# A row-maximum kernel whose ten long loads are each split into two transfers on two DMA queues

## The chip, the cores and the metric

The kernel runs on one core of a Trainium2 chip. The metric is the device time of one execution in microseconds (us); the median of three runs counts.

A core has a matrix engine (TensorE, PE in the profile), a vector engine (VectorE, DVE), an activation engine (ScalarE, ACT), a general engine (GpSimd, POOL) and an engine for synchronization (SyncE, SP). They run side by side and wait for each other by semaphores. Data comes from the main memory (HBM) into the on-chip memory (SBUF, 128 partitions) by 16 DMA engines. A transfer is handed to them by an instruction of some engine; the transfers of SP stand in one queue, those of ScalarE in another.

## What is computed

The maximum of each of 32 x 512 rows of 1024 floats:

```python
def setup_inputs():
    batch, seq, dim = 32, 512, 1024
    return {"x": np.random.randn(batch, seq, dim).astype(np.float32)}

def reference(x):
    return np.max(x, axis=-1).astype(np.float32)
```

The input has 67.1 MB and is read once. The output has 64 KB.

## The kernel before

**Tiling.** The 16384 rows are laid over 128 partitions, so each partition has 128 rows. In what follows "a row" is one row on each of the 128 partitions: 128 x 1024 floats, 512 KB. The rows come in loads of `n` rows each (`BLOCKS`, line 13): loads 0 to 10 have 2, 15, 16, 14, 11, 11, 10, 10, 8, 8 and 7 rows, loads 11 to 17 have 3, 3, 3, 2, 1, 1 and 1. The last two rows come in two pieces of columns each (`PIECES`, line 26), four transfers. Within a load each partition reads one contiguous run of `n` x 4 KB.

**The ring.** Loads go into a ring of 47 rows (`RING`, line 17) in SBUF, one after another. A load that does not fit before the end begins at the ring's start (line 112). So load 4 takes the place of loads 0 and 1, loads 5 and 6 the rest of load 1 and part of load 2, load 7 that of loads 2 and 3, load 8 that of load 4, load 9 that of loads 4 and 5, load 10 that of loads 5 and 6.

**The order.** `PLAN` (line 31) writes out the steps by hand. `dN` reduces load N on VectorE (`direct`, line 184, through `maximum`, line 77, one instruction at line 78); `pN` reduces a part of the columns of some rows (`partial`); `tN` and `bN` send the other columns another way: PE transposes them into PSUM (line 160), ScalarE copies them out (line 166), GpSimd reduces over the partitions (line 168), PE transposes the result back (line 178); `mN` merges the two; `fN` reduces a piece. Only some rows of loads 10, 13, 14 and 17 go that way (`SHARED`, line 20), so PE, ScalarE and GpSimd have work only near the end.

Before each step `issue()` (line 231) hands over all loads whose place in the ring has no reader left in the plan; `readers` (line 222) counts the steps that still read each load. The waits themselves are put in by the framework: a transfer waits until the reduce that read its place has finished. It also waits for an earlier transfer with the same completion semaphore; transfers take eight such semaphores in turn. When all loads are handed over, the four pieces follow (line 243).

All loads and pieces are issued from SP, in this order. On ScalarE there are a table load, the six copies of line 166 and at the end two transfers that store the result (lines 265 and 267).

Of the kernel before, what the change touches and what calls it, by code (L numbers as in the profile page):

```python
# [40 lines left out]
def kernel(  # L41
# [5 lines left out]
    nc = tc.nc  # L47
# [29 lines left out]
    def maximum(out, in_):  # L77
# [8 lines left out]
        out=colno, data0=ident, data1=ident, initial=-1.0, op0=ALU.add, op1=ALU.mult))  # L86
    in_turn("DVE", nc.vector.transpose(out=rowno, in_=colno[:, :32]))  # L87
    for q in range(1, P // 32):
        part = rowno[q * 32:(q + 1) * 32, 0:1]
        in_turn("DVE", nc.vector.tensor_scalar(  # L90
            out=part, in0=part, scalar1=float(q * 32), scalar2=None, op0=ALU.add))
    identity = in_turn("DVE", nc.vector.tensor_scalar(  # L92
        out=ident, in0=colno, scalar1=rowno[:, 0:1], scalar2=None, op0=ALU.is_equal))
# [41 lines left out]
    def rows(j):  # L135
        start, n, _, _ = loads[j]
        return ring[:, I + start * D:I + (start + n) * D].rearrange("p (i d) -> p i d", d=D)
# [90 lines left out]
    issued = 0  # L228
    behind = None

    def issue():
        nonlocal issued
        while issued < len(loads):
            start, n, src, _ = loads[issued]
            if any(readers[j] and s < start + n and start < s + k
                   for j, (s, k, _, _) in enumerate(loads[:issued])):
                return
            load = nc.sync.dma_start(out=rows(issued), in_=src)  # L238
            issued += 1
        if any(readers[j] and s < at + last + 1 and at < s + k for j, (s, k, _, _) in enumerate(loads)):  # L240
            return
        while pieces:
            nc.sync.dma_start(out=pieces[0][0], in_=pieces[0][1])
            pieces.pop(0)

    for step in PLAN:
        issue()
        kind, k = step[0], int(step[1:])
        if kind in "dp":
            (direct if kind == "d" else partial)(k)  # L250
            readers[k] -= 1
        elif kind == "t":
            turn(k)
            readers[chunks[k][0]] -= 1
        elif kind == "b":
            back(k)
        elif kind == "m":
            merge(k)
        else:
            inst = maximum(*tail[k])  # L260
            if behind is None:
                behind = inst
# [34 lines left out]
```

## Time and profile before

| | |
|---|---|
| median of 3 runs | 163.71 us (163.69 to 163.97) |
| span of the profiled execution, first to last instruction | 162.1 us |
| VectorE busy | 135.3 us |
| VectorE waiting for loads | 23.5 us in 4 waits |
| PE, ScalarE, GpSimd busy | 13.6, 6.3, 15.9 us |
| DMA, mean rate over the span | 414 GB/s |

The page gives no other time for the profiled execution than its span; some 1.6 us lie outside it in the runs. Each engine's groups of instructions are told by the line of the kernel that made them, with the operation and the tiles (`ring<-in_x_dram` is a load). SPq is SP's sequencer issuing transfers. The profile's times count from the first instruction of the span.

```profile
ring<-in_x_dram SPq DMA_DIRECT2D x1, 7680.0 KB, 22.6
ring<-in_x_dram SPq DMA_DIRECT2D x1, 7168.0 KB, 58.0
```

These two lines list transfers: load 1 (7680 KB) landed 22.6 us after its issue, load 3 (7168 KB), which stands two places behind it in the same queue, 58.0 us after.

### The profile page before, as it was taken

To read this page: it belongs to the slowest core of one execution; us is meant where nothing else is said; L and a number is where in the kernel's file an instruction comes from. 1 tells how busy PE (TensorE), PEld (TensorE's weight loads), DVE (VectorE), ACT (ScalarE), POOL (GpSimd) and SP (SyncE) were. 2 spreads that over 40 slices of the span, in tenths; PEclk is the share of its full clock that TensorE was granted. 3 is DMA by queue.
4 is the path that set the end of the run, shared out by engine and by line. 5 is a ranking of instruction groups with operands and counts; after the bars stand their busy time and mean duration, and the time that the engine had idled before them with its cause. 6 is when DMAs were issued, how large, how long until landed. Compare 5 with 4: busy or idle time off the path is not lost.

```text
span 162.1 us, 295 instructions
## 1 busy us (share of the span) xinstructions
PE 13.6 (8%) x76; PEld 11.7 (7%) x76; DVE 135.3 (83%) x33; ACT 6.3 (4%) x7; POOL 15.9 (10%) x10
## 2 busy tenths in 40 slices
PE   0000000000000000000000000000000000772942
PEld 0000000000000000000000000000000000762731
DVE  3500019998399999999999999996999999999994
ACT  3000000000000000000000000000000000241120
POOL 0000000000000000000000000000000000099791
PEclk9999999999999999999999999999999999996555
DMA  5995999599879999898999799799999989999991
GB/s 178 566 485 258 470 501 517 259 517 517 354 340 439 453 404 534 356 523 367 478 411 475 334 485 475 334 485 388 477 429 388 466 382 446 415 421 416 411 388 34
DMA packets 3456, 67.18 MB, mean 414 GB/s; under 512 B 640, under 2 KB 896, under 8 KB 1536
## 3 DMA queue, kind: packets, MB, share of 16 engines
q1 hardware_dynamic: 3168, 67.11, 96.8%
q10 hardware_dynamic: 288, 0.07, 0.2%
HBM read 67.11 MB, written 0.07 MB: 414 GB/s over the span
## 4 chain that ended last, share of the span: by engine, by line
DMA 50%; DVE 47%; SPq 1%; issue 0%; DVEq 0%
DMA ring<-in_x_dram 50%; DVE ring L78 45%; DVE joint L78 2%; SPq L238 1%; DVEq L292 0%
## 5 line engine op out<-in xcount | busy, mean ns | idle before, releaser
L78 DVE TENSOR_REDUCE ring<-ring 128x1 f32<-128x1024 f32 (+13 forms) x20 | 129.9, 6547 | 23.5 <-DMA ring<-in_x_dram 23.5
L168 POOL PARTITION_ALL_REDUCE top<-sb x6 | 15.7, 2658 | 142.6 <-ACT sb L166 142.5
L160 PE MATMUL ps<-ident,ring 128*128 128x128 f32 x38 | 9.0, 423 | 140.0 <-DMA ring<-in_x_dram 140.0
L160 PEld LDWEIGHTS ps<-ident,ring 128*128 128x128 f32 x38 | 7.6, 225 | 140.1 <-issue 140.1
L166 ACT COPY sb<-ps 128x1024 f32<-128x1024 f32 (+2 forms) x6 | 5.0, 834 | 150.5 <-PE ps L160 143.5
L78 DVE TENSOR_REDUCE joint<-ring 128x2 f32<-128x1280 f32 (+1 forms) x3 | 3.9, 1314 | 0.0
L178 PE MATMUL got<-ident,top 1*128 1x1 f32 x24 | 2.7, 228 | 3.8 <-POOL top L168 3.6
L178 PEld LDWEIGHTS got<-ident,top 1*128 1x128 f32 x24 | 2.4, 188 | 4.6 <-POOL top L168 4.6
L178 PE MATMUL joint<-ident,top 1*128 1x1 f32 x14 | 2.0, 244 | 1.9 <-POOL top L168 1.9
L178 PEld LDWEIGHTS joint<-ident,top 1*128 1x128 f32 x14 | 1.7, 210 | 2.7 <-POOL top L168 2.7
L166 ACT ACT_TABLE_LOAD x1 | 1.3, 1283 | 0.7 <-PEq L281 0.7
L83 DVE MEMSET ident<- 128x128 f32 x1 | 0.2, 165 | 0.8 <-PEq L281 0.8
L90 DVE TENSOR_SCALAR rowno<-rowno 32x1 f32<-32x1 f32 x3 | 0.4, 146 | 0.1
L85 DVE TENSOR_TENSOR_SCAN colno<-ident 128x128 f32<-128x128 f32 x1 | 0.4, 425 | 0.0
L92 DVE TENSOR_SCALAR ident<-colno,rowno 128x128 f32<-128x128 f32 x1 | 0.3, 288 | 0.0
L87 DVE STREAM_TRANSPOSE rowno<-colno 128x32 f32<-128x32 f32 x1 | 0.2, 211 | 0.0
L78 DVE TENSOR_REDUCE ring<-got 128x3 f32<-128x24 f32 x1 | 0.2, 172 | 0.0
L78 DVE TENSOR_REDUCE ring<-joint 128x5 f32<-128x20 f32 x1 | 0.2, 170 | 0.0
L281 POOL MEMSET const-float32-0.0<- 128x1 f32 x1 | 0.1, 98 | 0.2 <-issue 0.2
L281 POOL MEMSET const-bfloat16-1.0<- 128x1 bf16 x1 | 0.1, 102 | 0.0
L281 POOL MEMSET const-uint8-127<- 128x1 uint8 x1 | 0.1, 101 | 0.0
L281 POOL MEMSET const-float32-1.0<- 128x1 f32 x1 | 0.1, 98 | 0.0
(1 smaller groups left out, 0.1 us busy)
## 6 DMA issues: line engine op xcount, KB each, us to landing
ring<-in_x_dram SPq DMA_DIRECT2D x2, 5632.0 KB, 29.9
ring<-in_x_dram SPq DMA_DIRECT2D x2, 5120.0 KB, 36.8
ring<-in_x_dram SPq DMA_DIRECT2D x2, 4096.0 KB, 32.5
ring<-in_x_dram SPq DMA_DIRECT2D x1, 7680.0 KB, 22.6
ring<-in_x_dram SPq DMA_DIRECT2D x1, 7168.0 KB, 58.0
ring<-in_x_dram SPq DMA_DIRECT2D x3, 1536.0 KB, 35.7
ring<-in_x_dram SPq DMA_DIRECT2D x1, 3584.0 KB, 29.2
ring<-in_x_dram SPq DMA_DIRECT2D x2, 1024.0 KB, 17.8
```

The costliest lines, as they stand in the source:

```text
L78: return in_turn("DVE", nc.vector.reduce_max(out=out, in_=in_, axis=X))
L83: in_turn("DVE", nc.vector.memset(ident, 1.0))
L85: in_turn("DVE", nc.vector.tensor_tensor_scan(out=colno, data0=ident, data1=ident, initial=-1.0, op0=ALU.add, op1=ALU.mult))
L87: in_turn("DVE", nc.vector.transpose(out=rowno, in_=colno[:, :32]))
L90: in_turn("DVE", nc.vector.tensor_scalar(out=part, in0=part, scalar1=float(q * 32), scalar2=None, op0=ALU.add))
L92: identity = in_turn("DVE", nc.vector.tensor_scalar(out=ident, in0=colno, scalar1=rowno[:, 0:1], scalar2=None, op0=ALU.is_equal))
L160: in_turn("PE", nc.tensor.transpose(out=ps[:, w:w + P], in_=rows(j)[:, lead[j] + r + i, c * P:(c + 1) * P], identity=ident,))
L166: in_turn("ACT", nc.scalar.copy(out=sb[:, :W], in_=ps[:, :W]))
L168: in_turn("POOL", nc.gpsimd.partition_all_reduce(top[:, :W], sb[:, :W], P, bass_isa.ReduceOp.max))
L178: in_turn("PE", nc.tensor.transpose(out=share(j)[:, r + i, c:c + 1], in_=tops[k][0:1, w:w + P], identity=ident[0:1, 0:1],))
L238: load = nc.sync.dma_start(out=rows(issued), in_=src)
L281: nc = _bacc.Bacc("TRN2", target_bir_lowering=False, num_devices=1)
```

## The change

A load of more than six rows is issued as two transfers. SP issues the upper rows, `half` to `n`, and ScalarE's queue the lower `half` = `n // 2` rows. Both stand at the same place in `issue()`; the ring, the plan, the reduces and all other transfers stay. Loads 1 to 10 are concerned: SP takes 8, 8, 7, 6, 6, 5, 5, 4, 4 and 4 rows of them, ScalarE's queue 7, 8, 7, 5, 5, 5, 5, 4, 4 and 3. Loads 0 and 11 to 17 and the pieces stay whole on SP.

```diff
-            load = nc.sync.dma_start(out=rows(issued), in_=src)
+            half = n // 2 if n > 6 else 0
+            nc.sync.dma_start(out=rows(issued)[:, half:, :], in_=src[:, half:, :])
+            if half:
+                nc.scalar.dma_start(out=rows(issued)[:, :half, :], in_=src[:, :half, :])
             issued += 1
```

In the built program ScalarE's ten transfers come first in its stream, ahead of the table load and the copies.

## The prediction

> **What bounds the kernel now.** A "row" below is one row of x for each of the 128 partitions: 128 x 1024 floats, 512 KB. The kernel loads 128 of them. I read the busy line of each engine first, then the DMA queues, then the chain of waits, then VectorE's timeline.
>
> ```profile
> PE 13.6 (8%) x76; PEld 11.7 (7%) x76; DVE 135.3 (83%) x33; ACT 6.3 (4%) x7; POOL 15.9 (10%) x10
> q1 hardware_dynamic: 3168, 67.11, 96.8%
> DMA 50%; DVE 47%; SPq 1%; issue 0%; DVEq 0%
> ```
>
> Two things are nearly full: the 16 DMA engines (96.8% of the span by the packets of the one load queue) and VectorE (83%). The chain that ended last is half the one and half the other. The packet count tells how a load is cut: 22 loads make 3168 packets, 144 each, that is 128 of data (one for each partition, so 8 on each of the 16 engines, whatever the length) and 16 small ones that signal the end.
>
> ```profile
> 5.65 2.29 DVE L78 TENSOR_REDUCE ring<-ring 128x2 f32<-128x2048 f32 x1 [3.14 <-DMA ring<-in_x_dram]
> 23.78 16.15 DVE L78 TENSOR_REDUCE ring<-ring 128x15 f32<-128x15360 f32 x1 [15.85 <-DMA ring<-in_x_dram]
> 43.13 66.53 DVE L78 TENSOR_REDUCE ring<-ring 128x16 f32<-128x16384 f32 x5 [3.20 <-DMA ring<-in_x_dram]
> 110.97 40.23 DVE L78 TENSOR_REDUCE ring<-ring 128x10 f32<-128x10240 f32 x7 [1.30 <-DMA ring<-in_x_dram]
> ```
>
> This is the timeline of VectorE (start, length, what; in brackets the idle time before it). VectorE waits for load 0 (2 rows), for load 1 (15 rows), for load 2 (16 rows), then runs five reduces without a gap, waits 1.30 us for load 7, and from 110.97 works nearly without a gap to the end. Between the landings of loads 1 and 2 lie 16 rows and 43.13 - 23.78 = 19.35 us: 1.209 us a row for all engines together, 434 GB/s. All later landings follow from it, since the queue never runs dry.
>
> ```profile
> 43.13 66.55 DVE ring L78 x5
> 111.01 38.94 DMA ring<-in_x_dram
> 149.97 1.22 DVE ring L78
> 158.52 0.05 issue
> 158.57 0.49 DVE ring L78
> 159.05 0.09 issue
> 159.14 0.59 DVE ring L78
> ```
>
> These are pieces of the chain of waits. The last two pieces of data land just as VectorE is ready for them (0.05 and 0.09 us of waiting). So the end is set by both: data landing later ends later, and VectorE running late from load 2 on ends later too, less the 1.30 us before load 7 and these 0.14 us, which are all the slack it has.
>
> **The change part by part.** Loads 1 to 10 (15, 16, 14, 11, 11, 10, 10, 8, 8, 7 rows) become an upper part on SP (8, 8, 7, 6, 6, 5, 5, 4, 4, 4 rows) and a lower one on the Activation queue (7, 8, 7, 5, 5, 5, 5, 4, 4, 3 rows). Bytes, destinations and reduces are the same. In the built program's order the ten Activation transfers stand ahead of everything else on ScalarE.
>
> *Issuing.* SP issues the same 22 transfers; ScalarE issues ten more, at 0.33 to 0.61 us by the rows of L238, some 4 us in all. Queued behind them on ScalarE are the table load (1.28 us, at 0.72 until now) and the six copies of L166, and for these POOL and PE wait. The last Activation transfer (load 10) waits for the reduce of load 6, which ends at 109.67 now and near 118 by the forecast below; the first copy starts at 140.95. So 20 us cover it: cost 0. Without that cover it would be the 1.28 us.
>
> *Waits for semaphores.* Transfers share eight completion semaphores in turn, and each waits for the one eight places before it. With 32 in place of 22, loads 11 to 13 newly wait for load 7's two parts and load 8's upper part; the latest of them, 8's upper part, lands near 125 by the count below, when half of load 9 and loads 10 to 12 (4+7+3+3 = 17 rows, some 20 us) are still queued, so no engine runs dry. The four last pieces wait, as now, for loads 10 to 13. Each reduce waits for two semaphores: an added semaphore instruction is 0.017 us in the rows of L238. Together 0 to 0.1 us; I take 0.
>
> *DMA time.* The records of the packets in the trace give 2267 ns for 61,440 bytes, 1213 for 32,768, 1062 for 28,672 and 160 for 4,096: 27.1, 27.0, 27.0 and 25.6 bytes a ns, back to back. The halves are 12 to 32 KB long, a length that costs nothing. Ten more transfers at 8 packets and some 5 ns are 0.4 us at most, and only if the DMA still sets the end; I take 0. A gain in rate: an engine gives the same 27 whether its packet is 28 or 64 KB, so I see no gap that a second queue fills. Only the start has one. Load 2 ends 33 rows: 43.13 - 33 x 1.209 = 3.23, while the first packet starts at 1.73. At most those 1.5 us of warming up and signalling could be won.
>
> Here the Trainium skill speaks against a gain, and leaves the loss open. DMA: Bandwidth & Descriptors, section "Issuing engines are not separate DMA queues", says that issuing from several engines saves only issue time; on its own it would make this change cost nothing, 163.7. The section "Queues, rings and completion order" adds that an engine takes turns between queues a packet at a time, and that a packet is some 9 to 17 descriptors: with one packet to a descriptor that is the first way below, with a transfer's whole share as one packet it is the third. No run here shows which.
>
> *Order of landing.* This is the term that matters. A load is ready when both parts are; the Activation queue has no part of load 0, so it begins load 1 while SP is at load 0, and is ahead from then on. What it moves ahead is taken from the load that VectorE waits for. One queue only is busy in this trace, so how an engine shares is not shown, and the cost is bounded by the ways it could:
>
> 1. A packet from each queue in turn. Each transfer has 8 packets on an engine, so transfers pair up: load 0 (2 rows) with 1's lower part (7), 1's upper (8) with 2's lower (8), 2's upper (8) with 3's lower (7). Load 1 is complete after 2+7+8+8 = 25 rows instead of 17 and load 2 after 40 instead of 33. Load 1: 23.78 + 8 x 1.209 = 33.45, its reduce ends at 49.60. Load 2: 43.13 + 7 x 1.209 = 51.59, later than that, so it decides. If SP's packet goes first in each turn, the last packet of load 3's lower part (8.46/8 = 1.06 us) falls behind it; I take half of that, 0.53: 51.06. The five reduces take 66.53: 117.6, against 110.97 now, so +6.6; less the 0.14 at the end, **+6.5**.
> 2. Byte by byte. SP has 10 rows to the end of load 1 and 18 to the end of load 2, the other queue moves as many: 20 and 36 rows, each 3 late. +3.63 - 1.30 - 0.14 = +2.2.
> 3. A whole transfer in turn, SP first: 0, 1 lower, 1 upper, 2 lower, 2 upper: 17 and 33 rows, +0.
> 4. All of the Activation queue's first three transfers (22 rows) first: load 1 after 32 rows, 41.9, reduced by 58.07, when load 2 (40 rows) is there: 58.07 - 43.13 - 1.30 - 0.14 = +13.5.
>
> The nearest row is that of the packets themselves, which are recorded one after another at a length of one partition, so I take the first.
>
> *What is late next.* Nothing starves by it: load 4 is issued after load 1's reduce, 49.6, while the 47 rows before it last until 3.2 + 47 x 1.209 = 60; loads 5 and 6 after load 2's, 117.6 - 66.53 + 17.22 = 68.3, while load 4 lasts to 73; load 8 after load 4's, near 95, while load 7 lasts to 111. Later loads are shifted too (load 7 by load 8's lower 4 rows, 4.8 us, to 115.8), but VectorE comes for it at 117.6 only. From there the data is always earlier than VectorE, which sets the end alone.
>
> The sum: 162.1 + 6.5 = 168.6 of span. The runs before have a median of 163.71, 1.6 above the span: **170.2 us**.
>
> **The rivals.** *Byte by byte* (2): 163.71 + 2.2 = 165.9. For it: nothing says that an engine finishes one packet before it begins another queue's. Against: in its one queue no packet overlaps the next. *A whole transfer in turn* (3), the case on the other side: the place is each engine's choice between the two rings, the price 0, 163.7, and it decides if load 0 goes ahead of the other queue's first transfer on all 16 engines; if the other goes first, it becomes case 1. For it: both engines start at 0.72, and load 0 has short packets. Against: it needs all 16 engines alike. *A smaller lead*: if the Activation queue's first packet comes some microseconds after SP's, part of load 0 is done; with 2 of its 8 packets gone the lead is 6 of 8, 5.25 rows: 6.35 - 0.53 - 1.44 = +4.4, 168.1; with 4 gone 3.5 rows, +2.3. *A start-up gain*: up to 1.5 us off loads 1, 2 and 7 alike, with landings otherwise in order, 162.2. *The other queue first* (4): 177.2.
>
> **How the numbers follow.** A measurement of this kernel can tell 0.2% (0.33 us) from no change. Packet by packet with up to two packets of delay (168.1 to 170.9): 0.52, and its own range is that. A smaller lead (166.5 to 168.1): 0.09. Byte by byte (165.3 to 166.5): 0.19. Whole transfers, same time: 0.10. Start-up gain: 0.05. Other queue first: 0.05. The range takes the first three, 0.80: 165.2 to 171.2. Faster 0.05, same 0.10, slower 0.85.
>
> **What would show it.** VectorE's wait before load 1 grows from 15.85 to some 20 (load 0 itself is late, near 12) and load 1 starts near 33; load 2 starts near 51; the wait before load 7 is gone; from load 2 on VectorE has no gap; the load queues together still move 67.11 MB by 159. Starts near 27 and 47 would say byte by byte; 23.8 and 43.1 that nothing moved. The prediction is wrong if load 2 lands by 44.4 (the 1.30 us of slack then swallow it), if VectorE waits for a later load as well, or if the last data lands well ahead of 158.

## The result, and the profile after

The change makes the kernel slower: 171.03 us (median of 4 runs, 170.94 to 171.11) against 163.84 us for the kernel before beside it (163.69 to 163.97). The ratio is 1.0444, with a 95% interval of 1.0431 to 1.0456. The span of the profiled execution went from 162.1 to 169.2 us.

From the page of the kernel after: busy time by engine, the two DMA queues (q1 is SP's, q10 ScalarE's) and the chain that ended last.

```profile
PE 12.6 (7%) x76; PEld 11.0 (6%) x76; DVE 135.0 (80%) x33; ACT 6.3 (4%) x7; POOL 15.9 (9%) x10
q1 hardware_dynamic: 3168, 39.32, 55.1%
q10 hardware_dynamic: 1728, 27.85, 38.6%
DVE 47%; DMA 43%; issue 8%; DVEq 0%; SPq 0%
```

No engine does more work than before. The bytes are the same; q10 carries the ten lower parts and the stores. So the lost time is waiting: 30.8 us of VectorE's waiting for loads, against 23.5 before. (The 8% of "issue" in the chain are not idle time of VectorE, which the profile shows busy without a break from 85 to 150 us.) VectorE's timeline of the kernel after (start, length, what; idle time before it in brackets):

```profile
14.04 2.29 DVE L78 TENSOR_REDUCE ring<-ring 128x2 f32<-128x2048 f32 x1 [11.53 <-DMA ring<-in_x_dram]
33.55 16.15 DVE L78 TENSOR_REDUCE ring<-ring 128x15 f32<-128x15360 f32 x1 [17.22 <-DMA ring<-in_x_dram]
51.77 106.41 DVE L78 TENSOR_REDUCE ring<-ring 128x16 f32<-128x16384 f32 x12 [2.08 <-DMA ring<-in_x_dram]
158.10 3.02 DVE L78 TENSOR_REDUCE joint<-ring 128x2 f32<-128x1280 f32 x2
```

Load 0 starts on VectorE 8.4 us later than before (5.65), load 1 9.8 us later (23.78) and load 2 8.64 us later (43.13). From 51.77 on there is no bracket: twelve reduces follow each other without waiting. The 1.30 us of waiting before load 7 are gone, and VectorE alone sets the end from here.

Why load 2 is late can be read from the records of the single packets. The table shows, for the first transfers of each queue, when the first packet began, when the last one ended on the slowest engine, and when the small packets that signal the end ran (first and last engine):

| transfer, kernel after | rows | first packet | last data ends | signals |
|---|---|---|---|---|
| SP: load 0 | 2 | 1.73 | 12.58 | 13.32 to 13.64 |
| ScalarE: load 1, lower | 7 | 2.29 | 13.64 | 13.32 to 13.64 |
| SP: load 1, upper | 8 | 13.33 | 31.80 | 32.68 to 33.00 |
| ScalarE: load 2, lower | 8 | 14.54 | 33.01 | 32.69 to 33.01 |
| SP: load 2, upper | 8 | 32.69 | 50.16 | 50.88 to 51.22 |
| ScalarE: load 3, lower | 7 | 33.90 | 51.22 | 50.89 to 51.23 |

Before, load 0 ran from 1.73 to 5.28, load 1 from 4.81 to 23.39 and load 2 from 22.92 to 42.73. Now each SP transfer runs beside ScalarE's part of the next load, and their signals come together whatever their sizes: 8 packets of 8 KB (load 0) take as long as 8 packets of 28 KB, but for one turn (12.58 and 13.64). That is a packet from each queue in turn. A count of the data packets begun says the same: 96 in each queue by 10 us, 176 in each by 20 us, 256 in each by 32 us. Load 0 pays for 7 rows of load 1, load 1 for 8 rows of load 2, and load 2 for 7 rows of load 3.

### The profile page after: what moved, and what is told of

Its sections match the earlier page's. It is cut to its first block, busy times and chain, and to the rows that moved or that the text cites. A ratio compares the mean times of both kernels' runs of the same rounds, so it can differ in the third digit from the quotient of the medians.

```text
span 169.2 us, 320 instructions
## 1 busy us (share of the span) xinstructions
PE 12.6 (7%) x76; PEld 11.0 (6%) x76; DVE 135.0 (80%) x33; ACT 6.3 (4%) x7; POOL 15.9 (9%) x10
## 4 chain that ended last, share of the span: by engine, by line
DVE 47%; DMA 43%; issue 8%; DVEq 0%; SPq 0%
DVE ring L78 45%; DMA ring<-in_x_dram 43%; DVE joint L78 2%; DVEq L295 0%; SPq L239 0%; DVEq L78 0%
## 5 line engine op out<-in xcount | busy, mean ns | idle before, releaser
L78 DVE TENSOR_REDUCE ring<-ring 128x1 f32<-128x1024 f32 (+13 forms) x20 | 129.6, 6547 | 30.8 <-DMA ring<-in_x_dram 30.8
L160 PE MATMUL ps<-ident,ring 128*128 128x128 f32 x38 | 8.3, 396 | 140.2 <-DMA ring<-in_x_dram 140.2
L160 PEld LDWEIGHTS ps<-ident,ring 128*128 128x128 f32 x38 | 6.9, 211 | 140.3 <-issue 140.2
L166 ACT ACT_TABLE_LOAD x1 | 1.3, 1283 | 108.5 <-DVE ring L78 108.5
```

Source lines behind the costliest of these rows:

```text
L78: return in_turn("DVE", nc.vector.reduce_max(out=out, in_=in_, axis=X))
L160: in_turn("PE", nc.tensor.transpose(out=ps[:, w:w + P], in_=rows(j)[:, lead[j] + r + i, c * P:(c + 1) * P], identity=ident,))
L166: in_turn("ACT", nc.scalar.copy(out=sb[:, :W], in_=ps[:, :W]))
```

## The experiments

All are variations of the changed kernel, measured beside the kernel before, whose median in these runs is 163.75 (the first four) and 163.82 (the other four). Each moves the same rows to the same ring places; only the cut, the queue and in one case a wait differ.

**Both parts on SP.**

```diff
-                nc.scalar.dma_start(out=rows(issued)[:, :half, :], in_=src[:, :half, :])
+                nc.sync.dma_start(out=rows(issued)[:, :half, :], in_=src[:, :half, :])
```

> The same twenty halves, but both of each load issued from SP, one after the other. Theory (a queue's lead: packets of the two queues go in turn, and ScalarE's queue begins load 1 while SP is at load 0): no second queue, no lead; load 1 starts on VectorE at 23.8 and load 2 at 43.1 as before, and what remains is the price of ten more transfers at 8 packets of some 5 to 9 ns, 0.4 to 0.7 us: 163.9 to 164.5. Rival (cutting the loads is what costs: more packets, more completion semaphores taken in turn, reduces that wait for two signals): 170 or more.

Measured: 164.50 us, ratio 1.0046 (1.0033 to 1.0060). VectorE's timeline of this kernel:

```profile
23.67 16.15 DVE L78 TENSOR_REDUCE ring<-ring 128x15 f32<-128x15360 f32 x1 [15.98 <-DMA ring<-in_x_dram]
43.09 55.80 DVE L78 TENSOR_REDUCE ring<-ring 128x16 f32<-128x16384 f32 x4 [3.27 <-DMA ring<-in_x_dram]
99.11 10.82 DVE L78 TENSOR_REDUCE ring<-ring 128x10 f32<-128x10240 f32 x1 [0.22 <-DMA ring<-in_x_dram]
```

Loads 1 and 2 start as before the change. The cut alone costs 0.75 us: by the packet records the last data ends at 159.05 instead of 158.56, 0.05 us for each of ten added transfers (an estimate from these two ends), and VectorE waits a little for loads (0.22 us before load 6, which did not wait before). The rest of the change's 7.2 us needs the second queue.

**Load 0 cut as well.**

```diff
-            half = n // 2 if n > 6 else 0
+            half = n // 2 if n > 6 or not issued else 0
```

> As the change, but load 0 is cut as well, one row from each queue. Theory (lead): both queues have a part of every load, the parts of one load pair up packet by packet, so no queue runs ahead: load 0 ready near 5.6, load 1 near 24, load 2 near 43.3, total 163.9 to 164.6. Rival (two queues at once cost as such, by contention or by signals that wait a turn at the other queue's packet): 168 or more, with load 2 starting at 46 or later. Rival (engines share by bytes): SP has one row more of load 1, so loads 1 and 2 are 1 row, 1.2 us, late, and load 2 starts at 44.3.

Measured: 164.98 us, ratio 1.0073 (1.0060 to 1.0085). All eleven loads now run on two queues at once. Waits and VectorE's timeline of this kernel:

```profile
DVE ring L78 <- DMA ring<-in_x_dram: 24.0, 6, 16.1
```

```profile
5.41 2.29 DVE L78 TENSOR_REDUCE ring<-ring 128x2 f32<-128x2048 f32 x1 [2.90 <-DMA ring<-in_x_dram]
23.78 16.15 DVE L78 TENSOR_REDUCE ring<-ring 128x15 f32<-128x15360 f32 x1 [16.08 <-DMA ring<-in_x_dram]
43.24 55.80 DVE L78 TENSOR_REDUCE ring<-ring 128x16 f32<-128x16384 f32 x4 [3.31 <-DMA ring<-in_x_dram]
```

Load 2 starts 0.11 us later than before the change, not 8.64, and the waits are 24.0 us as against 23.5 before and 30.8 after. By the packet records the signals of the two parts of load 1 come together, at 22.78 to 23.15 and 22.78 to 23.16. So two queues at once, with all ten loads cut, cost hardly more than one queue with the same cuts: VectorE's last reduce ends at 160.37, against 160.32 in the run on one queue and 159.83 before. One row of load 0 moved to the other queue takes away six of the seven microseconds. The total is 0.4 us above the upper end of what was expected. The spans of its runs are some 0.9 us longer than those of the kernel before beside them (162.9 against 162.0); where the other 0.3 us, outside the span, come from stays open.

**ScalarE's first transfer held back until load 0 has landed.** (`in_turn` keeps ScalarE's transfers in their order. The dots stand for arguments and lines left out.)

```diff
+            load = nc.sync.dma_start(...)
+            if not issued:
+                landed = load
...
+                lower = in_turn("LOW", nc.scalar.dma_start(...))
+                if issued == 1:
+                    tc.add_manual_dep(lower.ins, landed.ins.name, SYNC, reason="behind load 0")
```

> As the change, but ScalarE's first transfer is issued only when load 0 has landed. Theory (lead): SP is at the start of load 1's upper part by then, the two parts of load 1 go side by side from there, and loads 1 and 2 start within 1.3 us (one packet of the other queue) of 23.8 and 43.1: total 163.9 to 165.3. Rival (two queues cost as such): 168 or more. Rival (the lead is made again later on, whatever the start): load 2 or 3 is waited for until 47 or later, 167 or more.

Measured: 166.12 us, ratio 1.0142 (1.0129 to 1.0156), above the range. VectorE's timeline, and above it the issue of ScalarE's transfers, of this kernel:

```profile
5.38 1.35 ACTq L244 DMA_DIRECT2D ring<-in_x_dram  x3
...
27.32 16.15 DVE L78 TENSOR_REDUCE ring<-ring 128x15 f32<-128x15360 f32 x1 [19.65 <-DMA ring<-in_x_dram]
46.28 66.52 DVE L78 TENSOR_REDUCE ring<-ring 128x16 f32<-128x16384 f32 x5 [2.81 <-DMA ring<-in_x_dram]
```

The expectation assumed that ScalarE's packets begin soon after the issue at 5.38. They begin at 9.51, when SP has sent four of the eight packets of its part of load 1. Now SP is the one that runs ahead: the signals of load 1's upper part come at 19.64 to 19.98, those of the lower part at 26.45 to 26.79. Load 1 is 3.54 us late, about three of SP's 1.213 us packets from load 2. This is the same mechanism with the other queue in the lead; what the expectation missed is the 4.1 us from issue to first packet.

**A quarter in place of half.**

```diff
-            half = n // 2 if n > 6 else 0
+            half = n // 4 if n > 6 else 0
```

> The lower part is a quarter of the rows in place of half (3, 4, 3, 2, 2, 2, 2, 2, 2, 1 on ScalarE's queue). Theory (packets in turn, lead): load 0 (2) pairs with 3 rows, load 1's upper 12 with 4, load 2's upper 12 with 3: load 0 ready after 5 rows, load 1 after 21 instead of 17 (23.78 + 4 x 1.209 = 28.6), load 2 after 36 instead of 33 (46.8): +3.63 - 1.44 = +2.2 to 2.5, total 166.0 to 166.4. Rival (shared by bytes): ScalarE's queue has moved all 10 of its first rows when SP has moved load 1: load 1 is ready after 24 rows, 32.2, load 2 is ready long before VectorE comes at 48.4, total near 169.1. Rival (a cost for each added transfer, whatever its size): 171.

Measured: 166.65 us, ratio 1.0176 (1.0162 to 1.0190). VectorE's timeline of this kernel:

```profile
28.82 16.15 DVE L78 TENSOR_REDUCE ring<-ring 128x15 f32<-128x15360 f32 x1 [17.21 <-DMA ring<-in_x_dram]
47.04 66.52 DVE L78 TENSOR_REDUCE ring<-ring 128x16 f32<-128x16384 f32 x5 [2.06 <-DMA ring<-in_x_dram]
114.01 39.98 DVE L78 TENSOR_REDUCE ring<-ring 128x10 f32<-128x10240 f32 x7 [0.45 <-DMA ring<-in_x_dram]
```

Load 1 starts at 28.82 (28.6 by packets in turn, 32.2 by bytes) and load 2 at 47.04 (46.8). Sharing by bytes is out. The total is 0.25 us above the range: load 2 is 0.24 later than the sum had it, and VectorE still waits 0.45 us for load 7, a wait that the sum had taken as gone.

**Three quarters.**

```diff
-            half = n // 2 if n > 6 else 0
+            half = n - n // 4 if n > 6 else 0
```

> The lower part is three quarters of the rows (12, 12, 11, 9, 9, 8, 8, 6, 6, 6 on ScalarE's queue). Theory (packets in turn, lead): load 0 (2) pairs with 12 rows, load 1's upper 3 with 12, load 2's upper 4 with 11: load 1 ready after 29 rows (38.3), load 2 after 44 instead of 33 (56.4): +13.3 - 1.44 = +11.9, total 175.3 to 176.3. Rival (shared by bytes): load 2 not waited for, later loads are, and much more: 180 or more. Rival (a cost for each added transfer): 171.

Measured: 175.87 us, ratio 1.0741 (1.0725 to 1.0757). VectorE's timeline of this kernel:

```profile
38.49 16.16 DVE L78 TENSOR_REDUCE ring<-ring 128x15 f32<-128x15360 f32 x1 [16.01 <-DMA ring<-in_x_dram]
56.66 106.41 DVE L78 TENSOR_REDUCE ring<-ring 128x16 f32<-128x16384 f32 x12 [2.01 <-DMA ring<-in_x_dram]
```

Both starts are within 0.3 us of the row counts (38.3 and 56.4). With 3, 7 and 11 rows of load 3 ahead of load 2's end, load 2 starts 3.9, 8.6 and 13.5 us late: 1.2 to 1.3 us a row.

**Load 1 alone.**

```diff
-            half = n // 2 if n > 6 else 0
+            half = n // 2 if issued == 1 else 0
```

> Only load 1 is cut. Theory (lead): its lower 7 rows go beside load 0, which is then ready near 13.5 instead of 5.6, but VectorE waits for load 1 anyway, and load 1 is complete after the same 17 rows: load 1 starts at 23.8, load 2 at 43.1, total 163.7 to 164.0. Rival (any transfer that runs beside another queue costs): a tenth of the change's loss or more, 164.5.

Measured: 164.07 us, ratio 1.0014 (1.0005 to 1.0024). VectorE's timeline of this kernel:

```profile
14.17 2.29 DVE L78 TENSOR_REDUCE ring<-ring 128x2 f32<-128x2048 f32 x1 [11.66 <-DMA ring<-in_x_dram]
23.96 16.16 DVE L78 TENSOR_REDUCE ring<-ring 128x15 f32<-128x15360 f32 x1 [7.50 <-DMA ring<-in_x_dram]
```

Load 0 is as late as in the change, and that costs next to nothing: VectorE's idle time before loads 0 and 1 together is 19.16 us, as against 18.99 before, and most of it now stands before load 0. The total is 0.25 us above the kernel before, which is small but clear of noise, and 0.07 above the range. What was moved ahead belongs to the load that is wanted next.

**Load 2 alone.** The condition is `issued == 2`.

> Only load 2 is cut. Theory (lead): its lower 8 rows go beside load 0 and so ahead of load 1, which is complete after 25 rows instead of 17 and starts at 33.4; its reduce ends at 49.6, load 2 has long landed: 49.6 - 43.13 - 1.44 = +5.0, total 168.6 to 169.0. Rival (the loss grows with the number of cut loads): a tenth of it, 164.5.

Measured: 168.89 us, ratio 1.0311 (1.0296 to 1.0327). VectorE's timeline of this kernel:

```profile
34.00 122.47 DVE L78 TENSOR_REDUCE ring<-ring 128x15 f32<-128x15360 f32 x13 [15.86 <-DMA ring<-in_x_dram]
```

One cut load costs 5 of the change's 7 us, if it is the wrong one: 8 rows of load 2 go ahead of load 1, which starts at 34.00 (33.4 by the row counts). Its reduce is followed by twelve more without a gap.

**Loads 4 to 10.** The condition is `4 <= issued <= 10`.

> Loads 4 to 10 are cut, 1 to 3 whole on SP. Theory (a queue that runs dry starts ahead): the lower 5 rows of load 4 are issued after load 1's reduce, near 40, on an idle queue, and pair with load 3, so load 3 lands up to 5 rows and a turn for its signal late, 65.5 to 66.8 instead of near 60; VectorE waits 5 to 6.5 us for it, then no more: total 167.5 to 169.6. Rival (the loss is a matter of the start of the kernel, of loads 0 to 2 alone): 163.8 to 164.6.

Measured: 168.93 us, ratio 1.0314 (1.0299 to 1.0329). VectorE's timeline, and the issue of ScalarE's first transfers, of this kernel:

```profile
39.89 0.92 ACTq L241 DMA_DIRECT2D ring<-in_x_dram  x2
43.06 17.22 DVE L78 TENSOR_REDUCE ring<-ring 128x16 f32<-128x16384 f32 x1 [3.20 <-DMA ring<-in_x_dram]
66.12 38.70 DVE L78 TENSOR_REDUCE ring<-ring 128x14 f32<-128x14336 f32 x3 [5.84 <-DMA ring<-in_x_dram]
```

Loads 0 to 2 are untouched, and the loss comes at load 3: ScalarE's queue, empty until then, takes turns from its first packet on (at 44.52, by the packet records), and what it has is load 4. VectorE waits 5.84 us for load 3, within the 5 to 6.5 expected, and 0.30 and 0.27 us for two later loads, where no wait was expected. So the loss is not a matter of the start. In these runs a load that stood whole in one queue was delayed where a later load's part ran beside it in the other: load 0 in the run of load 1 alone, load 1 in that of load 2 alone, load 3 here.

No run beats the kernel before. By its packet records all 16 engines work without a break from 2.6 to 157 us, so there was little time that a second queue could fill, and what it changed in these runs was the order.

## Why the prediction was right, and where it was off

- *What bounds the kernel.* Right. DMA and VectorE together set the end, and a late load 2 was passed on to the end but for the slack.
- *Issuing and waits for semaphores at no cost.* Right within what can be seen: on ScalarE the table load now runs at 108.5 and the first copy at 141.69, with 32 us of idle time before the latter, so the cover held. One reading behind it was wrong. ScalarE's last transfer, the lower three rows of load 10, was forecast to wait for the reduce of load 6, near 118. These rows lie in the place of load 5 alone, and the transfer was issued at 108.01, after load 5's reduce; SP's part of load 10, which also takes a place of load 6, was issued at 118.33. So the cover was wider than the 20 us of the forecast.
- *DMA time, 0 to 0.4 us.* The upper end was a little low for the cut alone: 0.5 us in the landing of the last data and 0.75 us in the total (the run on one queue). In the change it is hidden: the last data lands at 159.27 (158.56 before), while VectorE is 7 us behind it.
- *Order of landing, packets in turn.* This mechanism was right: load 2's delay less the slack is 6.9 of the 7.2 us. The packet records show it. Six experiments that change only which rows run ahead of which follow the row counts to within 0.7 us in the starts of the loads, with losses from 0.25 to 12 us in the total; in the seventh, the held kernel, the count had to be made anew with the late start of ScalarE's queue, which was seen only in its records.
- *Its size.* The sum said +6.5 and the runs say +7.19. The mis-sized term is the half packet of 0.53 us that was taken off because SP's last packet of load 2 would end before ScalarE's. That packet did end a turn earlier, at 50.16. But the packets that signal the end stand behind it in the same queue and take a turn of their own: they ran at 50.88 to 51.22, after ScalarE's last packet. So load 2 was late by the full 7 rows (8.46 us) and 0.18 more: it started at 51.77 instead of the predicted 51.06. From there to VectorE's last instruction it took 116.70 us before and 115.00 after, so the slack was 1.70 instead of 1.44; and the end behind that instruction grew from 2.27 to 2.43. 8.64 - 1.70 + 0.16 = 7.1, the difference of the spans. The result lies 0.13 us above the range that the prediction gave to packets in turn (168.1 to 170.9) and only 0.17 below the end of the whole range: the mechanism was right, and the sum was 0.7 us low.
- *VectorE's wait before load 1.* "Some 20" was wrong: it is 17.22. Load 0 itself started at 14.04 rather than near 12, again for the turn of its signal (data until 12.58, signals until 13.64).
- *What is late next.* Right: after load 2 VectorE waits for no load.
- *The rivals.* Bytes in turn fell with the quarter cut (28.82 against 32.2). Whole transfers in turn, the case of no change, fell with the packet records. The other queue first would have started load 1 at 41.9; it started at 33.55. A start-up gain did not come: the first packet starts at 1.73, as before. A smaller lead did not occur here, since both queues began within 0.6 us (1.73 and 2.29), but it is what the held kernel shows from the other side. (With four packets gone, the sum that the prediction gives for it comes to 166.0, outside the 166.5 to 168.1 it gives this rival.)

## What to carry to other kernels

Here one queue already kept the DMA engines busy (96.8% of the span), and a second one brought no rate, only another order: 413 GB/s over the span with all loads side by side, 414 before. Each engine took a packet from each queue in turn, so a short transfer in one queue waited for as many packets of the other, however long these were (load 0: 8 packets of 8 KB, done at 12.58 instead of 5.28). Before splitting loads over two queues, then, write down for each load how many rows land before it is complete, and put the loads side by side so that both queues work on the same load, the first small one included. Even so the split kernel was 1.2 us slower than the one with whole loads on one queue. A look at when each load is wanted tells which delay is nearly free (load 0 here, 8.5 us late for 0.25 us in all) and which is not (load 2, 8.6 us of which 7.2 reach the end).

## What was not expected of the hardware

- The signal of a transfer's end took its own turn between the queues. In the kernel after, load 2's data was complete at 50.16 and its last signal came at 51.22, one packet of the other queue (1.06 us) later; before, with one queue, both came at 42.7. The signal also cost its own queue a turn: in the held kernel the signal of SP's part of load 1 came at 19.64, and SP's next packet only at 20.71, one packet of ScalarE's (1.06 us) later.
- A queue that joined busy engines started late. ScalarE's first packet came 4.1 us after the start of its issue in the held kernel (5.38 to 9.51) and 4.6 us after in the one that cuts loads 4 to 10 (39.89 to 44.52), as against 1.6 us on idle engines at the start of the kernel after (0.72 to 2.29). In that time the engines worked on packets of the other queue, of 1.2 and 2.1 to 2.4 us each. That the engines had already taken these packets when ScalarE's arrived would explain it; this was not tested.
